# Column-divided products in groups, feed-forward units in pairs with 2 KB rows, compressed scores in float32r, and scheduler estimates with a margin

## The chip, the cores and the metric

The kernel runs on one core of one Trainium2 chip. The metric is the device time of one execution, in microseconds (us). The kernel before takes 1206.9 us (median of three runs, 1205.29 to 1207.57). In what follows PE is the matrix engine, DVE the vector engine, ACT the scalar engine, POOL is GpSimd, and SP is the engine whose queue issues the DMA transfers.

## The reference

Two layers work on 256 tokens of width 1024. Each layer is a half-step SwiGLU, token mixing, and a second half-step SwiGLU, each behind an RMS norm that is modulated by a vector `c`; a last RMS norm follows.

```
def swiglu(h, w_in, w_out):                    # w_in 1024 x 5632, w_out 2816 x 1024
    gate, up = jnp.split(h @ w_in, 2, axis=-1)
    return (jax.nn.silu(gate) * up) @ w_out

def token_mix(h, w_in, ...):                   # w_in 1024 x 3360
    (qkv, z, b_raw, a_raw, q_n, kc, vc, ks, vs, kw, vw, g_raw) = split_cols(h @ w_in, IN_SIZES)
    y_gdn = gated_deltanet(...)                # 4 heads of 128, triangular solves in chunks
    y_nsa = native_sparse_attention(...)       # 8 heads of 64, 2 groups of keys
    return jnp.concatenate([y_gdn, y_nsa], axis=-1) @ w_out

# in native_sparse_attention: compressed keys (15 of them), one of its three branches
sc = jnp.einsum("bgrqn,bngd->...", qb, k_cmp) * scale
p_cmp = masked_softmax(sc, cmp_end[None, :] <= t[:, None])
o_cmp = p_cmp @ v_cmp
```

The modulation (`ada_w`, 1024 x 9216 for each layer) is a product of one row, so that its weights are read once and used once. All is float32.

## The kernel before, in words

All weights are read from memory once, in one stream of tiles of 128 x 1024 floats (512 KB), into ten buffers `raw`. ACT rounds a tile to float32r (`hi`), DVE subtracts it from the tile (`lo`), and PE multiplies with both: a float32 product x·w is made of three float32r products, xh·wh, xl·wh and xh·wl, that add up in one PSUM bank. In the names of the profile a product `bank<-hh,lo` has the normed tokens' high part `hh` as the moving side and the weights' low part `lo` as the side that is loaded; `hl,hi` and `hh,hi` are the other two. There are four buffers each for `hi` and for `lo`, and eight PSUM banks of 128 x 512 floats.

The modulation's weights (`ada_w`) go through the same `raw` buffers, between the others; their products are made by DVE (`ada<-raw,cond,ada`), ACT and POOL (`adb<-adb,raw`), as a column sum that PE only finishes.

In the feed-forward part a unit is 256 columns of the gates and the same 256 of the values. Its four tiles (two halves of the rows, gates or values) have rows of 256 floats, 1 KB, in memory. A unit uses two banks, and `ffn_act` makes silu(gate) times value from each, split again into parts `aa`. The functions `split_mm` and `early_mm` issue the three products of one weight block directly behind each other:

```
        PE.matmul(o, wh, xh, start=first, stop=False, skip_group_check=True)
        PE.matmul(o, wh, xl, start=False, stop=False, skip_group_check=True)
        PE.matmul(o, wl, xh, start=False, stop=last, skip_group_check=True)
```

In the mixing part, products whose output has only 32 or 64 rows use a quarter or a half of the array's columns, and neighbours on other columns can run at once ("narrow" products below): the attention's values (`bank<-pt,vp`, 64 rows), sums over heads, the corners of the triangular inverses, the compression of keys, and the last step of the modulation. The scores with compressed keys (`bank<-KC,QS`) are float32 products of 16 columns; a mask is added by a product with the identity (`bank<-cmask,identb`).

The order of all this is not the order of the code. The kernel is first recorded; a list scheduler (`Program.schedule`, `forward`, `backward`, `estimate`) then walks through the recorded instructions along estimates of their times, picks for each engine the ready one with the longest way to the end, gives tiles their buffers, and issues everything in that order. So every instruction comes from one line of the profile, L546. The estimates decide the order on all engines, which queue in that order.

Of the kernel before, what the change touches and what calls it, by code (L numbers as in the profile page):

```python
# [6 lines left out]
F32 = mybir.dt.float32  # L7
# [40 lines left out]
def const_arrays():  # L48
    """Masks and index patterns that depend on the shapes alone."""
# [39 lines left out]
DMA_START, DMA_DONE, DMA_BYTES, DMA_RING = 1100, 950, 360.0, 8  # L89
# [20 lines left out]
class Instr:  # L110
    """A recorded instruction."""
# [5 lines left out]

    def operands(self):
        """(writes, access pattern) of each operand in memory."""
        for k, a in list(enumerate(self.args)) + list(self.kw.items()):  # L120
            if is_ap(a):
                yield k in (0, "out", "accum_out"), a
# [9 lines left out]
class LogicalTile:  # L132
    """A tile of the recorded program: one use of one of the slots of its tag."""
# [23 lines left out]


class Slots:
    """The slots of a tag. A tile may take one before tiles that precede it in the program only if all of them  # L160
    still get theirs when the rest of the program goes on in its own order."""
# [57 lines left out]
def wait_end(engine, end, other):  # L219
    """When an engine may reuse the place of a tile that another was done with at end."""  # L220
    if engine == "dma":
        return end + DMA_DONE
    return end + (REUSE[engine] if engine == other else HOP.get((engine, other), 200))


class Program:
    def __init__(self, tc, trace=None):
# [3 lines left out]
        self.in_order, self.last_dma, self.boost = False, None, 0  # L231
# [3 lines left out]
    # -- recording --  # L235
# [17 lines left out]
    def region(self, ap):  # L253
        """(tile, first partition, end, bits of the columns)"""
# [21 lines left out]
    def record(self, engine, fn, args, kw):  # L276
        x = Instr(len(self.instrs), engine, fn, args, kw)
# [5 lines left out]
        for w, r in sorted((u for u in uses if u[1]), key=lambda u: u[0]):  # L283
# [21 lines left out]
        if engine == "tensor":  # L305
            # products keep their order within a bank, as one start flag may stand for several of them
            b = args[0].tensor.name
            if b in self.last_pe:
                before.setdefault(self.last_pe[b], False)
            self.last_pe[b] = x  # L310
# [10 lines left out]
    def estimate(self, x):  # L321
        """Sets the time that the instruction holds its engine, and that of its transfer."""
# [3 lines left out]
        x.table, x.transfer = None, 0  # L326
# [96 lines left out]
    def forward(self):  # L423
# [28 lines left out]
        while len(order) < len(self.instrs):  # L452
# [29 lines left out]
            if switch(x):  # L482
                cost += TABLE_LOAD
                table = x.table[0]
# [1477 lines left out]
```

## Time and profile before

| | |
|---|---|
| median of three runs | 1206.9 us (1205.29 to 1207.57) |
| span of the profiled execution, from its first to its last instruction | 1203.7 us; the median lies 3.2 us above it |
| PE busy | 1160.3 us, 96% of the span |
| DVE busy | 958.1 us, 80% |
| ACT busy | 669.8 us, 56% |
| POOL busy | 219.6 us, 18% |
| read from memory | 256.09 MB, 215 GB/s over the span |

The profile has one execution. Engine times are busy times; matmuls are pipelined, so that one lasts longer in the trace than the distance to the next. How fast PE works is read from how many matmuls start in a stretch, or from the distance of two starts. The granted clock (PEclk) is the share of 2.4 GHz that PE got.

### The profile page before, as it was taken

The page shows a single profiled execution, that of the slowest core. Times are in us where ns is not written, and L with a number is a line of the kernel's source. Part 1 is how long each engine was busy: PE and PEld are TensorE (multiplying, and loading weights), DVE is VectorE, ACT ScalarE, POOL GpSimd, SP SyncE. Part 2 cuts the span into 40 slices and gives each one's busy share as a digit, 9 for nine tenths or more (in the row PEclk, how much of TensorE's full clock was granted, in tenths as well). Part 3 has the DMA queues.
Part 4 walks back from the last instruction along what each step waited for, and adds up shares of the span by engine and source line. Part 5 has one row for each costly group of instructions (what it writes and reads, how often), then busy time and mean ns, then how long its engine had stood idle before and what let it go on. Part 6 is the DMA issues. An engine that isn't in the chain of part 4 may idle for free.

```text
span 1203.7 us, 24132 instructions
## 1 busy us (share of the span) xinstructions
PE 1160.3 (96%) x9450; PEld 1080.6 (90%) x9451; DVE 958.1 (80%) x1716; ACT 669.8 (56%) x1177; POOL 219.6 (18%) x184
## 2 busy tenths in 40 slices
PE   8998989999999999999999999999999999999997
PEld 3698989997988899999999999998797879999997
DVE  3699899898987699988978877999998669855543
ACT  2456446555585556556545454556657556644444
POOL 2033343220001233113221110233100013200001
PEclk9999999999999999999999999999999999999999
DMA  9879999985424378987976887988562235756540
GB/s 333 292 218 313 293 303 308 287 254 171 132 54 123 118 225 294 301 272 227 319 224 187 284 265 221 314 283 283 157 192 55 71 102 181 255 172 193 181 145 36
DMA packets 230758, 259.89 MB, mean 216 GB/s; under 512 B 16130, under 2 KB 190836, under 8 KB 230644
## 3 DMA queue, kind: packets, MB, share of 16 engines
q1 hardware_dynamic: 230644, 258.35, 68.0%
q8 instruction: 74, 1.21, 0.4%
q14 instruction: 40, 0.33, 0.1%
HBM read 256.09 MB, written 2.23 MB: 215 GB/s over the span
## 4 chain that ended last, share of the span: by engine, by line
PE 72%; DVE 16%; DMA 4%; issue 3%; ACT 3%; POOL 1%; DVEq 0%; POOLq 0%; ACTq 0%; SPq 0%
PE bank L546 72%; DVE lo L546 7%; DVE ada L546 2%; ACT hi L546 2%; DMA raw<-in_ffn_w_out_dram 1%; DMA raw<-in_ada_w_dram 1%; DVE qT L546 1%; DVE aa L546 1%; POOL adb L546 1%; DMA raw<-in_ffn_w_in_dram 1%; DMA w<-in_cmp_w_k_dram 1%; DVE av L546 0%; DVE hl L546 0%; DVE KL L546 0%; DVE Pt L546 0%
## 5 line engine op out<-in xcount | busy, mean ns | idle before, releaser
L546 DVE TENSOR_TENSOR lo<-raw,hi 128x1024 fp32r<-128x1024 f32 (+3 forms) x340 | 420.2, 1254 | 119.6 <-ACT hi L546 86.4
L546 ACT ACTIVATE hi<-raw 128x1024 fp32r<-128x1024 f32 (+3 forms) x340 | 344.6, 1028 | 282.1 <-PE bank L546 233.2
L546 PE MATMUL bank<-hh,lo 128*128 128x256 f32 x1440 | 380.2, 285 | 10.4 <-DVE lo L546 10.3
L546 PE MATMUL bank<-hl,hi 128*128 128x256 f32 x1440 | 385.0, 284 | 0.6 <-DVE hl L546 0.6
L546 PE MATMUL bank<-hh,hi 128*128 128x256 f32 x1440 | 384.0, 283 | 1.6 <-ACT hi L546 1.0
L546 PEld LDWEIGHTS bank<-hh,lo 128*128 128x128 f32 x1440 | 260.2, 189 | 14.4 <-DVE lo L546 13.9
L546 PEld LDWEIGHTS bank<-hh,hi 128*128 128x128 f32 x1440 | 264.1, 189 | 4.7 <-issue 1.7
L546 PEld LDWEIGHTS bank<-hl,hi 128*128 128x128 f32 x1440 | 264.2, 189 | 1.2 <-DVE hl L546 0.8
L546 PE MATMUL bank<-aa,hi 128*128 128x256 f32 x1408 | 247.7, 281 | 2.9 <-ACT hi L546 2.5
L546 PEld LDWEIGHTS bank<-aa,hi 128*128 128x128 f32 x1408 | 212.5, 189 | 3.4 <-ACT hi L546 2.7
L546 PE MATMUL bank<-aa,lo 128*128 128x256 f32 x704 | 188.4, 283 | 8.5 <-DVE lo L546 8.5
L546 POOL TENSOR_TENSOR adb<-adb,raw 128x512 f32<-128x512 f32 x65 | 98.4, 1514 | 305.2 <-ACT raw L546 283.9
L546 PEld LDWEIGHTS bank<-aa,lo 128*128 128x128 f32 x704 | 129.5, 189 | 11.2 <-DVE lo L546 11.1
L546 DVE SCALAR_TENSOR_TENSOR ada<-raw,cond,ada 128x512 f32<-128x512 f32 x131 | 111.1, 848 | 4.5 <-DMA raw<-in_ada_w_dram 3.6
L546 POOL TENSOR_TENSOR nS<-nS,nsq 128x256 f32<-128x256 f32 x42 | 42.5, 1013 | 257.8 <-ACT nS L546 184.6
L546 ACT ACTIVATE aa<-av 128x256 fp32r<-128x256 f32 x88 | 36.0, 412 | 60.7 <-DVE av L546 60.5
L546 POOL TENSOR_TENSOR ada<-ada,adb 128x512 f32<-128x512 f32 x28 | 49.7, 1773 | 104.6 <-DVE ada L546 100.6
L546 PE MATMUL bank<-xl,hi 128*128 128x258 f32 (+1 forms) x224 | 62.3, 293 | 1.3 <-DVE xl L546 1.2
L546 PE MATMUL bank<-xh,hi 128*128 128x258 f32 (+1 forms) x224 | 60.5, 289 | 2.1 <-ACT xh L546 2.1
L546 PE MATMUL bank<-xh,lo 128*128 128x258 f32 (+1 forms) x224 | 61.4, 288 | 0.0
L546 DVE TENSOR_TENSOR aa<-av,aa 128x256 fp32r<-128x256 f32 x88 | 48.5, 554 | 10.9 <-ACT aa L546 10.9
L546 PEld LDWEIGHTS bank<-xl,hi 128*128 128x128 f32 x224 | 41.6, 190 | 7.1 <-issue 4.2
(308 smaller groups left out, 1620.9 us busy)
## 6 DMA issues: line engine op xcount, KB each, us to landing
raw<-in_ffn_w_in_dram SPq DMA_DIRECT2D x172, 512.0 KB, 4.8
raw<-in_ada_w_dram SPq DMA_DIRECT2D x144, 512.0 KB, 4.9
raw<-in_ffn_w_out_dram SPq DMA_DIRECT2D x64, 512.0 KB, 4.6
raw<-in_mix_w_in_dram SPq DMA_DIRECT2D x40, 512.0 KB, 5.0
raw<-in_ffn_w_out_dram SPq DMA_DIRECT2D x32, 384.0 KB, 4.3
raw<-in_mix_w_out_dram SPq DMA_DIRECT2D x8, 512.0 KB, 4.2
raw<-in_mix_w_out_dram SPq DMA_DIRECT2D x16, 256.0 KB, 4.5
raw<-in_mix_w_in_dram SPq DMA_DIRECT2D x8, 408.0 KB, 3.8
```

What stands on the lines that cost most here:

```text
L546: r = getattr(getattr(self.tc.nc, x.engine), x.fn)(*map(bind, x.args), **{k: bind(a) for k, a in x.kw.items()})
```

## The change

Five things change.

1. `split_mm` and `early_mm` become `split_products` and `early_products`: for all blocks of a weight tile first the two products with `hi`, then all products with `lo`.
2. The feed-forward units after the first ones go in pairs: 512 columns, four banks, tiles of 2 x 512 floats for each partition, so that a row in memory is 2 KB. 152 of the 172 loads of `ffn_w_in` have this form.
3. Narrow products are recorded as a group (`PE.together`), which the scheduler places as one.
4. The scores with compressed keys: keys in a high and a low part side by side (`KC`, made by ACT and DVE in place of copies by DVE), one float32r product of 32 columns for each head in place of a float32 one of 16, and the mask and the sum of both parts by two additions on DVE (`cs`) in place of the product with the identity. The queries' high and low part lie on different halves of the partitions, as before.
5. The scheduler's estimates: 12% on DVE's and ACT's, 8% on transfers, transfers by rows, costs for a pause of PE, for a change between full and narrow products, and for DVE beside POOL.

```
+SLACK = {"vector": 1.12, "scalar": 1.12, "gpsimd": 1.0, "sync": 1.08}
+REFILL, DIVIDE, SHARED = 100, 95, 500
...
+        x.port = (x.engine == "vector" and not psum and sum(free_size(a) > 64 for a in aps[1:]) > 1)
-            x.transfer = size / DMA_BYTES / min(1, run / 512)
+            x.transfer = size / run * (PACKET + run / PACKET_BYTES) / 16
...
+        x.cost *= SLACK.get(x.engine, 1)
+        x.transfer *= SLACK["sync"]
...
+            if x.port and clock["gpsimd"] > at:
+                cost += min(SHARED, clock["gpsimd"] - at)
             if x.engine == "tensor":
+                cost += (REFILL if at > clock["tensor"] + 20 else 0) + (DIVIDE if x.cols != cols else 0)
...
+    def together(self, body):
+        self.program.parts, whole = [], self.program.parts
+        body()
+        parts, self.program.parts = self.program.parts, None
+        self.program.record(self.name, "group", parts, {})
...
+        for u in range(single, 11, 2):
+            for h in range(2):
+                subs = [([dram("ffn_w_in", (l * 2 + i) * D * 2 * DFF + (2 * h + r) * 256 * 2 * DFF + s * DFF + u * 256,
+                               [[2 * DFF, 128], [128 * 2 * DFF, 2], [1, 512]])], (2, 512), "k c")
+                        for r in range(2) for s in range(2)]
+                w_item(("fp", l, i, u, h), subs)
...
+    def split_products(jobs):
+        for o, wh, _, xh, xl, first, _ in jobs:
+            PE.matmul(o, wh, xh, start=first, stop=False, skip_group_check=True)
+            PE.matmul(o, wh, xl, start=False, stop=False, skip_group_check=True)
+        for o, _, wl, xh, _, _, last in jobs:
+            PE.matmul(o, wl, xh, start=False, stop=last, skip_group_check=True)
...
+        for u in range(single, 11, 2):
+            qs = [bank() for _ in range(4)]
+            for h in range(4):
+                for s in range(2):
+                    wh, wl = take(("fp", l, i, u, h // 2), h % 2 * 2 + s)
+                    jobs = [[(qs[j][:, s * 256:(s + 1) * 256], wh[:, k, cut[j]], wl[:, k, cut[j]], hh[:, 2 * h + k],
+                              hl[:, 2 * h + k], h == 0 and s == 0 and k == 0, h == 3 and k == 1) for k in range(2)] for j in range(4)]
+                    for part in jobs if h == 3 and s == 1 else [sum(jobs, [])]:
+                        split_products(part)
+            for j in range(4):
+                ffn_act(2 * u + j, qs[j][:, 0:256], None, qs[j][:, 256:512], ah, al)
...
             for g in range(2):
                 for hf in range(2):
-                    V.tensor_copy(KC[hf * 64:(hf + 1) * 64, g], q[g * 64:(g + 1) * 64, 0:16])
+                    S.activation(KC[hf * 64:(hf + 1) * 64, g, 0], q[g * 64:(g + 1) * 64, 0:16], AF.Copy)
+                    V.tensor_tensor(KC[hf * 64:(hf + 1) * 64, g, 1], q[g * 64:(g + 1) * 64, 0:16],
+                                    fr(KC[hf * 64:(hf + 1) * 64, g, 0]), op=OP.subtract)
...
             def cmp_scores(b):
-                for r in range(4):
-                    for g in range(2):
-                        o = q[:, r * 32 + g * 16:r * 32 + (g + 1) * 16]
-                        PE.matmul(o, fr(QS[g][:, r, tok(b)]), KC[:, g], start=r == 0 and g == 0, stop=False, skip_group_check=True)
-                    PE.matmul(q[:, r * 32:(r + 1) * 32], identb, cmask[:, b], start=False, stop=True, skip_group_check=True)
+                def products():
+                    for r in range(4):
+                        for g in range(2):
+                            PE.matmul(q[:, (r * 2 + g) * 32:(r * 2 + g + 1) * 32], QS[g][:, r, tok(b)],
+                                      KC[:, g].rearrange("p y n -> p (y n)"), start=True, stop=True, skip_group_check=True)
+                PE.together(products)
+                V.tensor_tensor(qv, qp[:, :, 0], CC[:, C_CM + 32 * b:...], op=OP.add)
+                V.tensor_tensor(qv, qv, qp[:, :, 1], op=OP.add)
```

What the new order looks like on PE is shown at three places. The first is in the first feed-forward part, where PE multiplies unit after unit; numbers behind a name tell buffers apart, and `lo_1293` is made from `hi_1274`. Before:

```order
L546 MATMUL bank_1296<-hh_451,lo_1293 128x256
L546 MATMUL bank_1296<-hh_451,hi_1274 128x256
L546 MATMUL bank_1296<-hl_458,hi_1274 128x256
L546 MATMUL bank_1299<-hh_451,lo_1293 128x256
L546 MATMUL bank_1299<-hh_451,hi_1274 128x256
L546 MATMUL bank_1299<-hl_458,hi_1274 128x256
```

The product with `lo` stands directly behind the two with `hi` of its block, and those of the next block follow it. In the changed kernel, in the same part of the program on PE (`lo_1349` is made from `hi_1332`):

```order
L583 MATMUL bank_1174<-hh_425,hi_1332 128x256
L583 MATMUL bank_1174<-hl_430,hi_1332 128x256
L583 MATMUL bank_1142<-hh_425,lo_1349 128x256 x2
L583 MATMUL bank_1174<-hh_425,lo_1349 128x256 x2
L583 MATMUL bank_1142<-hh_425,hi_1354 128x256
L583 MATMUL bank_1142<-hl_430,hi_1354 128x256
```

The products with `lo` have moved behind all products with `hi` of their banks, in blocks.

The second place is PE in the first layer's mixing part, where the attention's values (`pt,vp`) begin. Before:

```order
L546 MATMUL bank<-KL,QS 128x256
L546 MATMUL bank<-pt,vp 64x128
L546 LDWEIGHTS identb
L546 MATMUL bank<-mask_qk,identb 128x2x128
L546 MATMUL bank<-pt,vp 64x128
L546 MATMUL bank<-CC,p 128x128 x4
L546 MATMUL bank<-pt,vp 64x128
L546 MATMUL bank<-CC,p 128x128
```

Each narrow product stands alone between full ones. In the changed kernel, at the first values of the same layer on PE:

```order
L583 MATMUL bank<-pct,VC 128x512
L583 MATMUL bank<-CC,p 128x128 x4
L583 MATMUL bank<-pt,vp 64x128 x4
L583 MATMUL bank<-qT,kT 128x256
L583 MATMUL bank<-CC,p 128x128
L583 MATMUL bank<-KH,QS 128x256
```

The four values of a unit have moved together.

The third place is PE at the first scores with compressed keys, in the same mixing part. Before:

```order
L546 MATMUL bank<-hl,hi 128x256
L546 MATMUL bank<-KC,QS 128x16
L546 LDWEIGHTS identb
L546 MATMUL bank<-cmask,identb 128x32
L546 MATMUL bank<-KC,QS 128x16 x2
```

In the changed kernel:

```order
L583 MATMUL bank<-hh,lo 128x256 x5
L583 MATMUL bank<-KH,QS 128x2x128
L583 MATMUL bank<-Vt,Pt 128x128 x4
L583 MATMUL bank<-KC,QS 128x32 x8
L583 MATMUL bank<-Vt,Pt 128x128 x4
```

The eight products of a block of tokens have moved together, and the products with the mask are gone.

## Rows read from the trace of the kernel before

**Rows 1.** The page's head and engines: busy us (share of the span) xinstructions.

```profile
span 1203.7 us, 24132 instructions
PE 1160.3 (96%) x9450; PEld 1080.6 (90%) x9451; DVE 958.1 (80%) x1716; ACT 669.8 (56%) x1177; POOL 219.6 (18%) x184
```

**Rows 2.** The page's chain that ended last, share of the span by engine.

```profile
PE 72%; DVE 16%; DMA 4%; issue 3%; ACT 3%; POOL 1%; DVEq 0%; POOLq 0%; ACTq 0%; SPq 0%
```

**Rows 3.** Stretches: PE, PEld, DVE, ACT, POOL busy (xinstructions), PEclk, DMA share, GB/s.

```profile
150.00:200.00 50.00, 44.48 (x354) 42.98 (x354) 47.24 (x65) 27.93 (x45) 20.13 (x13) 0.93 0.92 302
300.00:350.00 50.00, 49.42 (x458) 46.75 (x457) 44.73 (x138) 33.54 (x84) 0.40 (x4) 1.00 0.43 119
1050.00:1100.00 50.00, 50.00 (x430) 49.84 (x429) 28.23 (x40) 24.62 (x37) 0.00 (x0) 1.00 0.59 180
```

**Rows 4.** Waits of PE, whole run: us in total, times, longest.

```profile
PE bank L546 <- DVE lo L546: 19.1, 26, 2.1
PE bank L546 <- ACT hi L546: 3.4, 4, 2.5
```

**Rows 5.** Waits, from 60 to 250 us alone.

```profile
PE bank L546 <- DVE lo L546: 9.4, 9, 2.1
```

**Rows 6.** Timeline of PE: start, us, instruction xcount [idle before <-releaser].

```profile
172.12 0.28 PE L546 MATMUL bank<-hh,lo 128*128 128x256 f32 x1
174.88 0.50 PE L546 MATMUL bank<-aa,hi 128*128 128x256 f32 x2 [2.48 <-ACT hi L546]
...
177.09 0.58 PE L546 MATMUL bank<-hh,lo 128*128 128x256 f32 x1 [1.59 <-DVE lo L546]
177.46 0.41 PE L546 MATMUL bank<-hh,hi 128*128 128x256 f32 x1
177.68 0.41 PE L546 MATMUL bank<-hl,hi 128*128 128x256 f32 x1
```

**Rows 7.** Timeline of DVE, around the same time.

```profile
169.61 1.51 DVE L546 TENSOR_TENSOR aa<-av,aa 128x256 fp32r<-128x256 f32 x1
...
177.06 0.41 DVE L546 TENSOR_TENSOR aa<-av,aa 128x256 fp32r<-128x256 f32 x1
```

**Rows 8.** Stretches of 5 us, columns as in rows 3.

```profile
165.00:170.00 5.00, 5.00 (x45) 5.00 (x44) 4.49 (x6) 3.80 (x7) 3.64 (x4) 1.00 0.97 313
...
175.00:180.00 5.00, 3.41 (x16) 3.21 (x17) 5.00 (x8) 0.00 (x0) 0.34 (x1) 0.54 1.05 343
180.00:185.00 5.00, 5.00 (x42) 4.85 (x40) 3.48 (x5) 3.88 (x7) 0.95 (x1) 0.78 1.08 359
```

**Rows 9.** A group of PE by form: xcount | busy us, mean ns | idle before.

```profile
L546 PE MATMUL bank<-KC,QS 128*128 128x16 f32 x64 | 8.2, 251 | 0.0
```

**Rows 10.** Timeline of PE at scores with compressed keys.

```profile
320.93 0.18 PE L546 MATMUL bank<-cmask,identb 128*128 128x32 bf16 x1
320.96 0.60 PE L546 MATMUL bank<-KC,QS 128*128 128x16 f32 x4
321.40 0.18 PE L546 MATMUL bank<-cmask,identb 128*128 128x32 bf16 x1
```

**Rows 11.** Timeline of PE at values; a narrow product is two records.

```profile
355.58 0.43 PE L546 MATMUL bank<-pt,vp 128*64 128x128 f32 x2
355.95 0.66 PE L546 MATMUL bank<-CC,p 128*128 128x128 f32 x4
```

**Rows 12.** Timeline of PE at a whole unit of values.

```profile
385.98 0.66 PE L546 MATMUL bank<-pt,vp 128*64 128x128 f32 x8
386.57 0.39 PE L546 MATMUL bank<-KH,QS 128*128 128x256 f32 x1
386.79 0.28 PE L546 MATMUL bank<-KL,QS 128*128 128x256 f32 x1
```

**Rows 13.** DMA issues: xcount, KB each, us from issue to landing.

```profile
raw<-in_ffn_w_in_dram SPq DMA_DIRECT2D x172, 512.0 KB, 4.8
raw<-in_ada_w_dram SPq DMA_DIRECT2D x144, 512.0 KB, 4.9
```

More of the change, by code (lines that the diff above doesn't have):

```diff
@@ L116, in __init__ @@
         self.start = self.end = 0.0
+        self.parts = [Instr(i, engine, *x) for x in args] if fn == "group" else [self]
     def operands(self):
-        for k, a in list(enumerate(self.args)) + list(self.kw.items()):
-            if is_ap(a):
-                yield k in (0, "out", "accum_out"), a
+        for x in self.parts:
+            for k, a in list(enumerate(x.args)) + list(x.kw.items()):
+                if is_ap(a):
+                    yield k in (0, "out", "accum_out"), a
     def hop(self, other, data=True):
@@ L276, in record @@
     def record(self, engine, fn, args, kw):
+        if self.parts is not None:
+            self.parts.append((fn, args, kw))
+            return
         x = Instr(len(self.instrs), engine, fn, args, kw)
@@ L305, in record @@
         if engine == "tensor":
[L307 to L310, printed above, removed]
+            for b in {y.args[0].tensor.name for y in x.parts}:
+                if b in self.last_pe:
+                    before.setdefault(self.last_pe[b], False)
+                self.last_pe[b] = x
         if engine == "sync" and self.in_order:
@@ L321, in estimate @@
     def estimate(self, x):
+        if x.fn == "group":
+            for y in x.parts:
+                self.estimate(y)
+            x.cost, x.cols, x.table, x.transfer, x.port = sum(y.cost for y in x.parts), x.parts[0].cols, None, 0, False
+            return
         aps = [a for _, a in x.operands()]
@@ L451, in forward @@
         window, cold, busy = 0, True, {}
+        cols = 128
         while len(order) < len(self.instrs):
@@ L611, in full, with SINGLE @@
         return v.rearrange(f"p ({pat}) -> p {pat}", **dict(zip(pat.split(), shape)))
+    def SINGLE(l, i):
+        early = MID[2 * l + i] if l or i else EARLY
+        return early + (11 - early) % 2
     def ffn_in_items(l, i):
-        for u in range(11):
+        single = SINGLE(l, i)
+        for u in range(single):
             subs = [([dram("ffn_w_in", (l * 2 + i) * D * 2 * DFF + h * 512 * 2 * DFF + s * DFF + u * 256,
@@ L833, in fin, with columns @@
                 q = bank()
-                for j in range(4):
-                    PE.matmul(q[32 * j:32 * j + 32, 0:8], sel, ar.rearrange("p a c -> p (a c)")[:, j::4], start=True, stop=True)
+                def columns():
+                    for j in range(4):
+                        PE.matmul(q[32 * j:32 * j + 32, 0:8], sel, ar.rearrange("p a c -> p (a c)")[:, j::4], start=True, stop=True)
+                PE.together(columns)
                 c = slice(4 * p - 4, 4 * p + 4)
@@ L900, in trunk @@
     mask_qk = cst.tile([128, 128], BF16, name="mask_qk")
-    cmask = cst.tile([128, 2, 32], BF16, name="cmask")
     LM = cst.tile([128, 2, 128], U8, name="LM")
@@ L1075, in ffn_body @@
         if startup:
-            while items[st["next"][0]][1] != ("fi", 0, 0, EARLY):
+            while items[st["next"][0]][1] != ("fp", 0, 0, EARLY, 0):
                 produce()
@@ L1085, in ffn_body @@
         nst.pop("rbs")
-        for u in range(early, 11):
-            if between and 2 * u in between:
-                between[2 * u]()
+        single = SINGLE(l, i)
+        for u in range(early, single):
             qs = [bank(), bank()]
@@ L1354, in head_sums, with heads @@
                 q = bank()
-                for h in range(4):
-                    PE.matmul(q[h * 32:(h + 1) * 32, 0:T], ones[:, 0:32], sq[:, h], start=True, stop=True)
+                def heads():
+                    for h in range(4):
+                        PE.matmul(q[h * 32:(h + 1) * 32, 0:T], ones[:, 0:32], sq[:, h], start=True, stop=True)
+                PE.together(heads)
                 r = tmp([128, T], F32, "hs")
@@ L1770, in values, with products @@
                 b, r, y = units[u]
-                for j in range(2):
-                    for g in range(2):
-                        yy, kt, x = (j, 0, 2 * j + g) if b == 0 else (y, j, 2 * g + j)
-                        PE.matmul(O[b][g * 64:(g + 1) * 64, r * 128:(r + 1) * 128], vp[:, kt, yy, g], pt[:, x * 128:(x + 1) * 128],
-                                  start=False, stop=j == 1 and (b == 0 or y == 1), skip_group_check=True)
+                def products():
+                    for j in range(2):
+                        for g in range(2):
+                            yy, kt, x = (j, 0, 2 * j + g) if b == 0 else (y, j, 2 * g + j)
+                            PE.matmul(O[b][g * 64:(g + 1) * 64, r * 128:(r + 1) * 128], vp[:, kt, yy, g], pt[:, x * 128:(x + 1) * 128],
+                                      start=False, stop=j == 1 and (b == 0 or y == 1), skip_group_check=True)
+                PE.together(products)
             def norm_out(b):
@@ L1784, in norm_out, with heads @@
                 q = bank()
-                for r in range(4):
-                    PE.matmul(q[r * 32:(r + 1) * 32, 0:128], BO, osq[:, r * 128:(r + 1) * 128], start=True, stop=True)
+                def heads():
+                    for r in range(4):
+                        PE.matmul(q[r * 32:(r + 1) * 32, 0:128], BO, osq[:, r * 128:(r + 1) * 128], start=True, stop=True)
+                PE.together(heads)
                 sr = tmp([128, 128], F32, "nsr")
```

143 lines of the change are left out of this document (75 added, 68 removed).

## The prediction

> **What bounds the kernel now.** I read the page's engines first: PE is busy for 1160.3 of 1203.7 us [rows 1], and the chain that ended last is 72% PE, 16% DVE and 4% DMA [rows 2]. So time is won where PE idles or works slowly, and hardly anywhere else. A busy PE may still be slow, so next come the stretches: in the second layer's last feed-forward part 430 matmuls start in 50 us, one each 50/430 = 0.116 us, and nothing holds PE up; from 150 to 200 us it is 354 [rows 3]. In that stretch DVE is busy for 47.2 of 50 us and the DMA share is 0.92: PE is fed by engines that are nearly full. The list of PE's waits says by whom: 19.1 us on `lo`, in 26 waits, and 3.4 us on `hi` [rows 4]; 9.4 of the 19.1 us lie between 60 and 250 us [rows 5]. The rest of the forecast is about four things: these waits, the clock that one of them costs, narrow products, and the compressed scores.
>
> **Compressed scores.** Before, 64 records of `KC,QS` [rows 9]. Four of them take 321.40 - 320.96 = 0.44 us, so 0.11 each, and a mask product 0.03 [rows 10]. There are 16 of these (four for each of two blocks of tokens, two layers): 64 x 0.11 + 16 x 0.03 = 7.5 us. After: 32 float32r products of 32 columns, which the trace doesn't show. They lie between 0.03 (the mask's 32 columns) and 0.116 (256 columns of float32r), so 1.0 to 3.7 us together. I take 0.11, the step of the same loaded side (`QS`, 128 columns) with few columns: 3.5 us. **4.0 us** saved, bounds 3.8 to 6.5. They count in full, since PE is busy for 49.4 of 50 us around them [rows 3]. ACT's eight roundings of `KC` and DVE's eight small additions lengthen the way to the scores; PE's projection products cover that. Without this cover, four blocks would each wait for two more short DVE instructions, 0.41 us or less each [rows 7]: 3 us.
>
> **Narrow products.** Counting along PE's order, narrow products come in 123 runs between full ones before, and in 89 after: 34 excursions fewer. A lone narrow product takes 355.95 - 355.58 = 0.37 us until the next full one starts [rows 11]. Four together take 386.57 - 385.98 = 0.59 us, 0.15 each, and the first full one behind them takes 0.22 in place of 0.116, so that a way back costs 0.10 [rows 12]. An excursion less thus saves 0.37 - 0.15 = 0.22 us: **7.5 us** for 34. Bounds: 0.10 each (the way back alone), 3.4 us, and 0.37 each, 12.6 us. These matmuls stand in PE's own queue, so the saving is on the path wherever PE has other work, and the mixing part has (49.4 of 50 us).
>
> **`lo` behind all of `hi`.** A DVE subtraction for a whole tile takes some 1.2 us, and PE now asks for `lo` eight products (median over 344 tiles, by PE's order) after the first use of `hi`, in 85 tiles at most two products after it. In the changed order it is 15 products, and for no tile fewer than three. Fifteen products are 15 x 0.116 = 1.7 us, against a mean wait of 19.1/26 = 0.73 us [rows 4]. So a wait for `lo` goes where DVE has time and was merely asked too early. That holds for the 19.1 - 9.4 = 9.7 us outside of 60 to 250 us, which I count in full. In 60 to 250 us DVE is full, and a product that waits less for `lo` soon waits for the next `hi`: of the 9.4 us I count a quarter, 2.3 us. **12.0 us**; bounds 0 (all waits move to `hi`) and 19.1. What is queued behind a product with `lo` is all of PE, as before. `hi` buffers come free earlier and `lo` buffers no later, so ACT isn't held longer.
>
> **The clock.** At 172.1 to 177.1 us PE waits 2.48 us for `hi` and 1.59 us for `lo` [rows 6]. Then the granted clock is 0.54 and 0.78 in two stretches of 5 us [rows 8], which is half speed (1.2 GHz) for part of each: two matmuls start 0.22 us apart [rows 6]. Work lost: 5 x 0.46 + 5 x 0.22 = 3.4 us. Why the waits came: DVE instructions take 1.51 us that otherwise take 0.41 [rows 7], while POOL is busy for 3.64 of 5 us [rows 8]. The Trainium skill (GPSIMD Engine Reference, Specifications) says that POOL's interfaces to on-chip memory are shared with DVE and that DVE instructions with two inputs there contend. This trace agrees, with 1.10 us added to `aa<-av,aa`; by the rule the change, which only lets its planner reckon with 0.5 us for it, leaves the contention, and the sum would lack the term that follows. From the rows alone: the new order puts other instructions side by side, so that this stall is gone or not with even chances; I take half of the loss, **1.7 us**, bounds 0 and 3.4 + 2.5 (with the wait for `hi`).
>
> **2 KB rows.** A load of 512 KB lands in 4.8 us with 1 KB rows (`ffn_w_in`) and in 4.9 us with 2 KB rows (`ada_w`) [rows 13]. I count 0. The loads lie beside PE's work except where the DMA share is above 0.9; 2% (4.9 against 4.8) of the 150 us between 100 and 250 is 3 us to either side.
>
> **Pairs and margins.** A pair holds four of eight banks, so that the next one can start in the other four; 0. The margin and all else that the new order brings has no row. PE idles 43.4 us in all [rows 1], of which 22.5 are the waits in rows 4; I count 0, and bound it by half of the other 21 us, 10 us to either side.
>
> **Sum.** 4.0 + 7.5 + 12.0 + 1.7 = 25.2 us. 1203.7 - 25.2 = 1178.5 us of span, and 3.2 us for the distance of span and median: 1182 us.
>
> **Rivals.**
>
> *DVE sets the pace.* Then all waits for `lo` become waits for `hi`, and the clock falls as before: only 4.0 + 7.5 us remain, 1195 us. For it: DVE's 47.2 of 50 us at 150 to 200, and that PE's longest wait in this part is for `hi` [rows 3, 6]. Against it: half of the waits lie where DVE has time (28 of 50 us busy in a quiet stretch) [rows 3]. 22%.
>
> *More goes than I count.* All waits for `lo`, the clock and its wait for `hi`, and 3 us by faster loads: 4.0 + 7.5 + 19.1 + 5.9 + 3 = 39.5, 1167 us. For it: fewer pauses feed on themselves, since each one makes the buffers that DVE and ACT wait for come free later. 17%.
>
> *Banks, slower than before.* There are 20 pairs, five in each feed-forward part. If a norm, a modulation column or the last unit still holds a bank when a pair starts, PE waits until ACT and DVE have emptied it, and PE's queue holds all behind that product. At the longest wait for `lo` seen, 2.1 us [rows 4], that is 42 us against 25 gained: 1224 us. It decides from 25.2/20 = 1.3 us for each pair on. Against it: the banks of the pair before last are 192 x 0.116 = 22 us old by then, and ACT has 44% of its time idle [rows 1]. 11%.
>
> *Nothing comes of it.* The new order loses elsewhere what these terms gain (the bound of 10 us and the DVE rival together): within 0.2% of before, which is about what a measurement of this kernel can tell from no change, 1204.5 to 1209.3. 5%.
>
> **Chances.** The forecast, 1174 to 1190 us, has 45%; with 22, 17, 11 and 5% for the rivals that is all. Faster: 45 + 22 + 17, less 2 for the tail of the DVE rival that ends near 1205: 82%. Same: 6%. Slower: 12%. Eight in ten: from 1164, below the second rival's value, to 1204, which takes in the first rival and its spread of 10 us; what is left out is the slow side and a little of the fast one.
>
> **What would show it.** In the profile after: the sum of PE's waits for `lo` falls from 19.1 to some 7 us, and those for `hi` stay under 10; there are 32 records of `KC,QS` and no `cmask`, with starts 0.11 us apart; values come as eight records in 0.6 us; no stretch after the first 50 us has a granted clock below 1; the stretch of 150 to 200 us starts 380 matmuls or more where it had 354. Wrong would be: waits for `hi` or for transfers of 15 us and more, a wait of PE for ACT or DVE at the start of pairs, or as many matmuls per stretch as before.

## The result and the profile after

On one chip the changed kernel took 1188.4 us (median of 4 runs, 1187.5 to 1190.1) and the kernel before 1207.2 us (4 runs): a ratio of 0.985, with an interval of 0.983 to 0.986. The forecast was 1182 us, with a range of 1174 to 1190 (45%) and a wider one of 1164 to 1204 (eight in ten); the measured time lies in both. The profiled execution has a span of 1186.8 us; before it was 1203.7.

The head and the engines of the page, and its chain by engine, as in [rows 1, 2]:

```profile
span 1186.8 us, 24089 instructions
PE 1143.4 (96%) x9402; PEld 1075.6 (91%) x9403; DVE 946.6 (80%) x1723; ACT 669.0 (56%) x1185; POOL 224.0 (19%) x184
...
PE 77%; DVE 11%; issue 4%; ACT 3%; DMA 3%; POOL 2%; DVEq 0%; POOLq 0%; SPq 0%; ACTq 0%
```

PE is busy 17 us less, as much as the span is shorter, and DVE holds 11% of the chain in place of 16%. That looks like a plain success of PE's side. It isn't one, as a table by stages shows. A stage ends with the last product of a feed-forward part (the last with `aa`) or of a mixing part (the last with `yh`); the columns are us, PE busy (xmatmuls), PEclk, DMA share, GB/s. Before:

```profile
0.00:250.10 250.10, 233.15 (x1763) 0.98 0.91 295
250.10:424.20 174.10, 170.26 (x1417) 1.00 0.46 134
424.20:623.40 199.20, 194.59 (x1618) 1.00 0.83 269
623.40:821.80 198.40, 192.77 (x1621) 1.00 0.82 261
821.80:1002.40 180.60, 176.18 (x1414) 1.00 0.47 138
1002.40:1194.70 192.30, 190.44 (x1605) 1.00 0.53 165
```

After:

```profile
0.00:233.10 233.10, 226.16 (x1772) 1.00 0.92 312
233.10:415.20 182.10, 170.05 (x1391) 0.97 0.44 130
415.20:610.70 195.50, 191.58 (x1612) 1.00 0.83 277
610.70:802.00 191.30, 190.84 (x1621) 1.00 0.81 265
802.00:988.30 186.30, 173.10 (x1391) 0.95 0.47 141
988.30:1177.60 189.30, 188.70 (x1604) 1.00 0.51 165
```

The second and the fifth line are the mixing parts. The four feed-forward parts together fell from 840.0 to 809.2 us, 30.8 us. The two mixing parts rose from 354.7 to 368.4 us, 13.7 us, although PE has less to do there. PE idles 25.2 us there (368.4 - 343.2) where it idled 8.3. And the granted clock is 0.97 and 0.95 in place of 1.00: in six stretches of 27.3 us together it is at half speed (1.2 GHz). PE is busy for 25.7 us of these, so that its busy time would be some 330 us at full speed (an estimate, 343.2 - 25.7/2), against 346.4 before. PE's own work in the mixing parts thus fell by some 16 us, and idle time and clock took more than that.

PE's waits, whole run (us in total, times, longest), answering [rows 4]:

```profile
PE bank L583 <- ACT hh L583: 5.2, 7, 1.7
PE bank L583 <- DVE hT L583: 3.3, 2, 2.6
PE bank L583 <- DVE av L583: 2.7, 2, 1.5
PE bank L583 <- DVE lo L583: 2.3, 4, 1.2
...
PE bank L583 <- ACT hi L583: 1.9, 4, 0.6
```

The wait for `lo` is almost gone (19.1 before), and the one for `hi` has not taken its place (3.4 before). Many small waits for other tiles, most of them in the mixing parts, have come. The stretches of [rows 3]:

```profile
150.00:200.00 50.00, 46.43 (x397) 45.49 (x396) 48.17 (x72) 29.18 (x48) 21.81 (x14) 1.00 0.94 310
300.00:350.00 50.00, 46.98 (x438) 41.93 (x438) 45.11 (x135) 38.25 (x105) 0.60 (x6) 0.97 0.24 67
...
1050.00:1100.00 50.00, 50.00 (x426) 50.00 (x426) 27.57 (x33) 23.83 (x33) 0.00 (x0) 1.00 0.58 187
```

From 150 to 200 us 397 matmuls start where it was 354, with DVE and the transfers as full as before: PE isn't fed by a faster DVE there; the same work is laid out differently in time. From 300 to 350 us, where the prediction saw PE busy for 49.4 of 50 us and so counted each saved product, it is now busy for 47.0 (the mixing part starts 17 us earlier, so that this is not quite the same piece of it).

Compressed scores and values, by PE's timeline (start, us, instruction xcount); before in [rows 10 to 12]:

```profile
315.44 1.04 PE L583 MATMUL bank<-KC,QS 128*128 128x32 f32 x8
316.33 0.36 PE L583 MATMUL bank<-Vt,Pt 128*128 128x128 f32 x1
...
341.01 0.66 PE L583 MATMUL bank<-pt,vp 128*64 128x128 f32 x8
341.60 0.70 PE L583 MATMUL bank<-qT,kT 128*128 128x256 f32 x2
```

Eight scores in 0.89 us, 0.11 each, and four values (eight records) in 0.59 us.

What a pause in a mixing part looks like now, in the second layer. PE's timeline (in brackets idle time before it, and what ended it):

```profile
895.77 0.45 PE L583 MATMUL bank<-Tt,NT 128*32 128x32 f32 x16
896.79 0.45 PE L583 MATMUL bank<-Tt,NT 128*32 128x32 f32 x16 [0.58 <-ACT Tt L583]
...
899.37 0.73 PE L583 MATMUL bank<-Vt,Pt 128*32 128x32 f32 x16 [0.94 <-ACT Pt L583]
...
902.16 1.09 PE L583 MATMUL bank<-CC,Vt 128*128 128x128 f32 x4 [0.58 <-DVE csm L583]
```

The chain of waits in the same place (start, us, what):

```profile
897.97 1.07 ACT sq L583
...
899.05 0.27 ACT Pt L583
...
899.64 0.32 ACT pc L583
...
899.98 0.29 DVE csm L583
900.27 1.13 DVE lo L583
901.40 0.03 issue
901.43 0.29 DVE Vt L583
```

And two stretches (columns as in [rows 3]):

```profile
895.00:900.00 5.00, 3.24 (x73) 2.41 (x71) 4.61 (x15) 4.73 (x10) 0.00 (x0) 1.00 0.00 0
900.00:905.00 5.00, 4.42 (x33) 3.12 (x28) 4.35 (x11) 1.58 (x3) 0.00 (x0) 0.71 0.34 111
```

PE idles while ACT and DVE (4.73 and 4.61 of 5 us busy) pass short steps of the triangular inverses (`Tt`, `Pt`, `Vt`) and of the attention (`pc`, `csm`) to each other; a square of 1.07 us on ACT and a weight tile's subtraction of 1.13 us on DVE stand in that chain's way. Behind the pause the granted clock falls to 0.71.

### The profile page after: what moved, and what is told of

The parts are those of the page before. It is cut to its first block, busy times and chain, and to the rows that moved or that the text cites. A ratio compares the mean times of both kernels' runs of the same rounds, so it can differ in the third digit from the quotient of the medians.

```text
span 1186.8 us, 24089 instructions
## 1 busy us (share of the span) xinstructions
PE 1143.4 (96%) x9402; PEld 1075.6 (91%) x9403; DVE 946.6 (80%) x1723; ACT 669.0 (56%) x1185; POOL 224.0 (19%) x184
## 4 chain that ended last, share of the span: by engine, by line
PE 77%; DVE 11%; issue 4%; ACT 3%; DMA 3%; POOL 2%; DVEq 0%; POOLq 0%; SPq 0%; ACTq 0%
PE bank L583 77%; DVE lo L583 4%; DMA raw<-in_ada_w_dram 1%; DVE ada L583 1%; DVE kT L583 1%; ACT hi L583 1%; POOL nS L583 1%; DMA raw<-in_mix_w_in_dram 1%; DVE hl L583 1%; POOL adb L583 1%; DVE Pt L583 1%; DVE gm L583 0%; DVE aa L583 0%; DVE NT L583 0%; DVE nt L583 0%
## 5 line engine op out<-in xcount | busy, mean ns | idle before, releaser
L583 PE MATMUL bank<-hh,hi 128*128 128x256 f32 x1440 | 355.1, 284 | 2.4 <-ACT hh L583 1.8
L583 PE MATMUL bank<-hl,hi 128*128 128x256 f32 x1440 | 351.0, 284 | 0.1
L583 PE MATMUL bank<-hh,lo 128*128 128x256 f32 x1440 | 274.2, 285 | 2.2 <-DVE lo L583 2.1
L583 PEld LDWEIGHTS bank<-hh,lo 128*128 128x128 f32 x1440 | 217.2, 190 | 5.3 <-DVE lo L583 3.0
L583 PE MATMUL bank<-aa,hi 128*128 128x256 f32 x1408 | 205.7, 281 | 4.2 <-DVE av L583 2.7
L583 PEld LDWEIGHTS bank<-aa,hi 128*128 128x128 f32 x1408 | 185.7, 189 | 5.1 <-issue 3.0
L583 POOL TENSOR_TENSOR adb<-adb,raw 128x512 f32<-128x512 f32 x65 | 104.8, 1613 | 314.4 <-ACT raw L583 272.0
L583 PE MATMUL bank<-aa,lo 128*128 128x256 f32 x704 | 125.1, 282 | 0.5 <-DVE lo L583 0.2
L583 PEld LDWEIGHTS bank<-aa,lo 128*128 128x128 f32 x704 | 102.5, 188 | 1.6 <-DVE lo L583 1.5
L583 ACT ACTIVATE raw<-raw,cond 128x512 f32<-128x512 f32 x65 | 44.4, 712 | 7.0 <-DMA raw<-in_ada_w_dram 6.7
```

Source lines behind the costliest of these rows:

```text
L583: r = getattr(getattr(self.tc.nc, y.engine), y.fn)(*map(bind, y.args), **{k: bind(a) for k, a in y.kw.items()})
```

## The experiments

Feed-forward and mixing are sums of the four and two stages, in us; `lo` is PE's wait for `lo`, changes are those from a full to a narrow product in the mixing parts. The end, 9 to 10 us in all of them, is left out.

| kernel | ratio to before, interval | feed-forward | mixing | lo | changes |
|---|---|---|---|---|---|
| before | 1 | 840.0 | 354.7 | 19.1 | 89 |
| after | 0.985, 0.983 to 0.986 | 809.2 | 368.4 | 2.3 | 59 |
| e1_lo_behind_hi | 1.010, 1.008 to 1.013 | 839.1 | 367.1 | 14.8 | 95 |
| m_planner_alone | 1.010, 1.007 to 1.012 | 823.2 | 384.2 | 4.1 | 105 |
| e4_interleaved | 0.994, 0.992 to 0.996 | 828.4 | 361.6 | 11.7 | 52 |
| e7_oldest | 1.006, 1.004 to 1.008 | 846.1 | 355.4 | 24.5 | 54 |
| e3_nomargin | 1.006, 1.004 to 1.008 | 826.6 | 377.7 | 10.1 | 59 |
| b_margins_alone | 1.005, 1.004 to 1.006 | 835.6 | 366.0 | 5.0 | 52 |
| e2_nogroup | 1.006, 1.004 to 1.008 | 813.4 | 388.9 | 1.9 | 126 |
| e5_singles | 0.983, 0.981 to 0.984 | 814.3 | 361.2 | 3.3 | 53 |
| j_margin_111 | 0.990, 0.988 to 0.991 | 816.0 | 369.1 | 8.7 | 52 |
| b_margin_120 | 0.982, 0.980 to 0.983 | 818.1 | 357.1 | 2.5 | 58 |
| f1_same_places | 1.175, 1.171 to 1.179 | 996.7 | 405.0 | 29.5 | 87 |
| f4_same_places | 1.347, 1.344 to 1.350 | 1175.8 | 440.2 | 187.0 | 61 |

How far the plan itself is a throw of dice was asked of j_margin_111:

```
-SLACK = {"vector": 1.12, "scalar": 1.12, "gpsimd": 1.0, "sync": 1.08}
+SLACK = {"vector": 1.11, "scalar": 1.11, "gpsimd": 1.0, "sync": 1.08}
```

> The kernel after with the margins of DVE and ACT at 1.11 in place of 1.12: a step too small to mean anything by itself, to see how far planning anew moves the time. If each planning is a throw, it lands anywhere from 1183 to 1200 us, with the mixing parts 5 us or more from 368; the single differences of 5 to 10 us between the other kernels then tell nothing. If it is within 2 us of 1188, they tell something.

1195.5 us, 7 us more than after, for a step of 0.01. The feed-forward parts moved by 6.8 us, the mixing parts by 0.7. The mixing parts alone are no steadier: in after, j_margin_111, b_margin_120 and e5_singles, which differ in a margin or in the feed-forward parts only, they take 357.1 to 369.1 us, 12 us apart. So a difference of 7 us in time, or of 12 us in the mixing parts, between two kernels that were planned anew says nothing of the edit by itself; what follows rests on larger differences, or on several pairs of kernels that agree.

**What took the waits for `lo` away.** The new order of products alone, in the kernel before (e1_lo_behind_hi):

```
+        for o, wh, _, xh, xl, first, _ in jobs:
             PE.matmul(o, wh, xh, start=first, ...)
             PE.matmul(o, wh, xl, start=False, ...)
-            PE.matmul(o, wl, xh, start=False, stop=last, ...)
+        for o, _, wl, xh, _, _, last in jobs:
+            PE.matmul(o, wl, xh, start=False, stop=last, ...)
```

> The kernel before with one edit: in the units of weights, all products with hi stand ahead of those with lo. Theory A (the new order of products took away the waits for lo and, with them, most of the 30.8 us that the feed-forward parts gained): the feed-forward parts, 840 us before, come to 815 to 825, PE's waits for lo fall from 19 to under 5 us, the time to about 1187 to 1194. Theory B (the planner's new estimates, margins and price for contention took them away): feed-forward parts stay within 5 us of 840, time 1202 to 1210. Theory C (the pairs with 2 KB rows took them away): as B. The mixing parts stay at 355 us by A; if they rise to 362 or more here too, their loss of 13.7 us does not come from groups or margins.

```profile
PE bank L546 <- DVE lo L546: 14.8, 21, 1.5
```

Theory A failed: 1220 us, feed-forward parts as before, and `lo` is still waited for. PE asks later, and the planner puts the subtraction later too: from the end of ACT's `hi` to the end of DVE's `lo` of the same tile it is 1.52 us in the kernel before (median over 344 tiles, paired in order) and 2.21 us here. In the two kernels below it is 1.53 (old order of products, new estimates) and 1.50 (e4_interleaved).

In the kernel after it is 2.19 as well, although PE hardly waits there, so that this median doesn't tell what took the waits away. The room tells more, from the end of a tile's `lo` on DVE to PE's first product with it (paired by the order in which each kernel's own scheduler issues them). It is 0.1 us or less for 36 of the 344 tiles before, and still for 31 here, for 36 in e7_oldest and for 45 in e3_nomargin, which all plan without margins. In the eight kernels with margins that were planned in the usual way it is so for 8 to 24 tiles, 12 of them in the kernel after.

The mixing parts rose to 367.1 us here, with nothing but the order of products changed. By the test that the expectation set (362 or more), what the kernel after loses there need not come from groups or margins.

The planner's estimates alone, in the kernel before (m_planner_alone):

```
+REFILL, DIVIDE, SHARED = 100, 95, 500
+SLACK = {"vector": 1.12, "scalar": 1.12, "gpsimd": 1.0, "sync": 1.08}
...  (and the times of transfers and of narrow products)
```

> The kernel before with the planner's new estimates, price for contention and margins, and none of the other edits. Theory P: feed-forward parts fall from 840 to 825 or 830 us, about as in the kernel after with the old order of products (828), waits for lo to about 12 us. Theory A (the order of products is what pays): they stay within 5 us of 840. The mixing parts have no groups here: if groups are worth 20 us there, they rise to 375 or more; if not, 355 to 368.

```profile
PE bank L558 <- DVE lo L558: 4.1, 11, 1.0
```

Theory P came true in the main: waits for `lo` fall to 4.1 us, further than the 12 expected, and the feed-forward parts by 16.8 us, with the old order of products. The kernel is slower all the same, by 29.5 us in its mixing parts, which have no groups; 375 us or more there was to mean that groups are worth some 20 us under these estimates.

The kernel after with the old order of products (e4_interleaved: the first diff the other way), and with all of the old estimates (e7_oldest):

> The kernel after with the old order of products (hi, lo and hi with the other half of the weights in turn, tile by tile). Theory A: waits for lo come back, 10 to 19 us of them, and the time rises by 10 to 20 us to 1198 to 1208, all of it in the feed-forward parts. Theories B and C: within 5 us of 1188. If the margins leave enough room ahead of lo, it is B.

> The kernel after with all of the planner's estimates as they were before (no margins, no price for contention or for changing between full and narrow products, the old times of transfers and of narrow products); products, groups, pairs and compressed scores stay. Theory A (order of products): feed-forward parts at 820 us or less. Theory P (it is the order and the plan together): 825 to 840, as with the margins alone taken away (827). In the mixing parts: if the new estimates are what makes PE wait there, they come to 350 us or less, time about 1185; if the groups leave PE with less work than the chain of DVE and ACT takes, they stay at 365 to 380, time 1200 to 1220.

```profile
PE bank L583 <- DVE lo L583: 24.5, 22, 2.9
```

e4_interleaved loses 19.2 us in the feed-forward parts, as theory A wanted, and gains 6.8 us in the mixing parts, which it didn't; e7_oldest, which has every edit but the estimates, loses 36.9 us in the feed-forward parts, more than either theory allowed, and waits more for `lo` than the kernel before. Read as a square, the feed-forward parts take 840 us with neither, 839 and 846 with the order of products alone, 823 and 828 with the estimates alone, and 809 to 818 with both (five kernels). By the means (840, 842.6, 825.8 and 814.2) the estimates are worth 14 us with the old order of products and 28 with the new one. The order is worth some 12 us, with 5 us between the nearest two kernels, and only under the new estimates.

Which of the estimates? The margins taken away (e3_nomargin, all of `SLACK` at 1.0), and the margins alone (b_margins_alone, the other estimates as before):

> The kernel after with the margins on the planner's times set to 1.0. Theory M (the margins spread the mixing parts' work so that PE waits and its clock falls): the mixing parts fall from 368 to about 357 us and the time to about 1177. Theory B (the margins are what keeps PE from waiting in the feed-forward parts): the feed-forward parts rise from 809 to 820 or more, time 1198 or more. By the prediction, which counted the margins at nothing: 1184 to 1193.

> The kernel after with the margins, but with all other estimates of the planner as they were before (no price for contention or for changing between full and narrow products, the old times of transfers and of narrow products). So far the feed-forward parts took 809 to 818 us wherever the new estimates and the new order of products came together, 827 without the margins and 846 with no new estimate; the mixing parts took 355 us with the old estimates and 357 to 369 with the new ones (378 with the new ones without margins). Theory Q (the margins help the feed-forward parts, the other estimates harm the mixing parts): feed-forward 812 to 822, mixing 352 to 360, time 1176 to 1188, the fastest so far. Rival R (the margins themselves stretch the mixing parts, or the other estimates are needed in the feed-forward parts too): mixing 362 or more, or feed-forward 825 or more, time 1190 to 1210.

Without the margins the feed-forward parts lose 17.4 us, without the others 26.4. So both are needed there. Theory M failed, since the mixing parts rose without the margins, to 377.7 us, and theory Q, that the others could be left out, failed too: 1213 us. Against e7_oldest, which has neither, the margins alone take the waits for `lo` from 24.5 to 5.0 us, but only 10.5 us off the feed-forward parts; the others alone take 19.5 us off them. Which of the others does it was not taken apart. One of them, the price for DVE beside POOL, doesn't do what its name says: `aa<-av,aa` takes 0.42 us (median) or up to 1.53 us in the kernel after (count, shortest, median and longest in ns):

```profile
L583 DVE TENSOR_TENSOR aa<-av,aa x88: 403/420/1531, 72.2 to 1124.0; 128x256 fp32r<-128x256 f32 x88
```

It takes over 0.6 us in 14 of 88 cases before, in 13 after, and in 9 in e7_oldest, which has no such price: the long cases stay. In these three kernels each of them lies beside busy time of POOL. By the rule that the prediction took from the Trainium skill (GPSIMD Engine Reference, Specifications) they would; the trace agrees.

Two kernels were to take the planner out: they put the products of a piece of weights into the places that the plan of the other order of products had given them, with every other engine's queue as it was. f1_same_places does this in the kernel before, f4_same_places in the kernel after:

```
+    for y in dst.instrs:
+        if y.unit is not None:
+            pos[y] = units[y.unit].pop()      # the unit's own places, in the new order
...
+        # where the places would wait for each other, the next product that can go takes its turn
+        y = min(can, key=lambda y: pos[y]) if can else next(x for x in reversed(queues["tensor"]) if before[x] <= done)
```

> The kernel before with the new order of products, but not planned anew: every instruction of the other engines keeps its place in its queue, and the products of a piece of weights share the places that they had, those with lo last. Theory A (asking later for lo pays by itself): PE's waits for lo fall from 19 to under 5 us, the feed-forward parts from 840 to about 828 us, the mixing parts stay at 355 us, time 1192 to 1197. Theory P (the order pays only where the planner has left DVE room): the waits go over to hi and to others, feed-forward parts stay within 3 us of 840, time 1203 to 1210. In both, the 12 us that planning the same edit anew cost in the mixing parts do not come.

> The kernel after with the old order of products (hi, hi, lo in turn), not planned anew: all else keeps its place. Theory A: waits for lo of 10 us or more come back, feed-forward parts rise from 809 to 820 or more, time 1198 to 1206. Theory P: the margins have put DVE's subtractions so early that hardly a wait comes back; within 4 us of 1188.

Both were far off, 1417 and 1627 us. PE's waits in f4_same_places:

```profile
PE bank L583 <- DVE lo L583: 187.0, 153, 8.2
```

They don't measure the order of products: where places were in each other's way other products moved too, and PE's queue is a different one throughout. The 153 waits of 1.2 us for `lo` speak against theory P too, which had hardly a wait come back, but with PE's queue so different that isn't shown. What the order of products would bring in an unchanged plan stays open.

**Pairs with 2 KB rows.** The kernel after with units one by one (e5_singles):

```
-        return early + (11 - early) % 2
+        return 11
```

> The kernel after with units one by one and rows of 1 KB. Theory C (pairs and longer rows carry a part of the feed-forward parts' gain): these rise from 809 by 10 us or more. By the prediction, which gave them nothing: they stay within 5 us of 809. The mixing parts may move by some 10 us either way, as planning anew has moved them so far.

1186.8 us, 0.983 against 0.985 for after, and feed-forward parts of 814.3 us, 5.1 us more. Theory C, which wanted 10 us or more, failed; 5 us are less than what planning anew moves. A load of `ffn_w_in` lands in 5.1 us there and in 4.7 us in the kernel after; PE waits for none of them in either.

**The mixing parts.** The kernel after without groups (e2_nogroup):

```
     def together(self, body):
-        self.program.parts, whole = [], self.program.parts
         body()
-        parts, self.program.parts = self.program.parts, None
-        self.program.record(self.name, "group", parts, {})
```

> The kernel after without the groups: narrow products are planned one by one. By the prediction's term (34 excursions of 0.22 us) it is 7.5 us slower, 1196, with about 120 changes from full to narrow products where the kernel after has 89. Theory G (groups hold PE in the mixing parts, which is where the half clock and the 13.7 us come from): it is faster by 5 to 10 us, 1178 to 1184, with mixing parts under 360 us and less than 14 us at half clock.

```profile
235.20:423.90 188.70, 183.80 (x1391) 0.99 0.43 127
...
812.00:1012.20 200.20, 189.83 (x1391) 0.97 0.45 133
```

1215 us. Theory G failed: groups don't hold PE up, without them the mixing parts take 20.5 us more. Counted from the first narrow product to the next full one, over the whole run, PE spends 72.6 us in 123 runs of narrow products before, 66.5 us in 88 runs after, and 93.1 us in 166 runs here. PE's idle time within these runs, 3.6, 8.5 and 10.0 us, is counted in. Under the new estimates the planner breaks ungrouped products up more than it did before (126 changes in the mixing parts against 89), and groups cure that.

Against the kernel before, no gain is left. e7_oldest has groups and the new compressed scores with the old estimates; its mixing parts:

```profile
252.60:425.50 172.90, 164.03 (x1398) 1.00 0.46 138
...
825.30:1007.80 182.50, 170.54 (x1391) 0.96 0.47 140
```

PE is busy for 334.6 us in place of 346.4, 11.8 us less, and idles 20.8 us in place of 8.3: the sum is 355.4 us, as before (354.7), and between what the two theories had for it. But e7_oldest has the new order of products too, which the kernel before lacks. The mixing parts of the three kernels that stand beside it, e1_lo_behind_hi, m_planner_alone and e4_interleaved, two lines each:

```profile
247.20:433.30 186.10, 178.12 (x1414) 0.99 0.45 131
834.80:1015.80 181.00, 175.78 (x1415) 1.00 0.48 141
...
241.80:429.60 187.80, 177.80 (x1418) 1.00 0.44 126
816.70:1013.10 196.40, 185.78 (x1409) 0.97 0.44 129
...
247.90:428.20 180.30, 167.33 (x1392) 0.98 0.45 131
818.60:999.90 181.30, 169.69 (x1391) 0.96 0.48 142
```

With the order of products and the estimates equal, groups and new scores (and pairs, which don't touch these parts) do show in the time: 11.7 us from e1_lo_behind_hi to e7_oldest, 22.6 us from m_planner_alone to e4_interleaved, and 20.5 us for the groups alone, from e2_nogroup to the kernel after. What took the gain, as far as these pairs tell, is the plan. The new order of products costs the mixing parts 12.4 us (before to e1_lo_behind_hi) and 6.8 (e4_interleaved to after), the new estimates cost them 29.5 (before to m_planner_alone) and 13.0 (e7_oldest to after). The smaller of these differences lie within or near the 12 us that planning anew moves these parts; but the three savings agree, and so do the four costs.

In all eight kernels with groups that were planned in the usual way PE idles some 20 us or more in the mixing parts, and none of them has these parts shorter than before: they take 355 to 378 us. The idle time isn't the groups' doing alone, since m_planner_alone idles 20.6 us there and e2_nogroup 15.3 without them. Why the new order and the new estimates make the plan of the mixing parts worse was not taken apart.

**A larger margin** (b_margin_120, 1.20 for DVE and ACT):

> The kernel after with the margins of DVE and ACT at 1.20 in place of 1.12. From 1.00 to 1.12 the time fell from 1215 to 1188 us. If room ahead of DVE's and ACT's results is what counts, it falls a little more, to 1178 to 1187, with less than 17 us of PE's waits and half clock in the mixing parts; if 1.12 has taken all there was, 1186 to 1195.

1186.2 us, the lowest median of all, with the mixing parts at 357 us. The time came as expected, but the sign that was to show why did not: PE idles 20 us in the mixing parts, with a clock of 0.99 and 0.97, where less than 17 us of waits and half clock together were expected. It and e5_singles lie below the kernel after in their medians, by 2.2 and 1.6 us and so by less than the 7 us that a meaningless step moves; no reason is claimed for them.

## Why the prediction was right, and where it was not

The time, the sign and the main place (waits for `lo` in the feed-forward parts) were right. The way to the number was half wrong: the feed-forward parts gained 30.8 us where 13.7 were counted, and the mixing parts lost 13.7 us where 11.5 were counted as gained. The sum came out near by luck, because errors of 17 us (feed-forward) and 25 us (mixing) had opposite signs.

*Compressed scores, 4.0 us.* The work was sized rightly: 32 records at 0.11 us, 3.5 us in place of 7.5. That they "count in full, since PE is busy for 49.4 of 50 us around them" was argued from a plan that didn't stay: in the changed kernel PE idles 25.2 us in the mixing parts. No run has the old scores with all else new. Together with the groups they show in the time between kernels of equal order and estimates (11.7 and 22.6 us, for 11.5 counted), and not against the kernel before.

*Narrow products, 7.5 us.* 34 excursions at 0.22 us were counted; measured are 35 runs fewer and 72.6 - 66.5 = 6.1 us, 0.17 each. Without PE's idle time inside the runs it is 69.06 - 58.02 = 11.04 us, 0.32 each, and against an ungrouped program under the same planner (83.1 - 58.0)/78 = 0.32 as well. So the work on PE was sized too low, within its bounds.

*`lo` behind all of `hi`, 12.0 us.* The effect was forecast as 19.1 down to some 7 us of waits; it was 2.3. The cause was given wrongly. "A wait for `lo` goes where DVE has time and was merely asked too early" supposes that DVE's place in the order stays when PE asks later. The planner moves DVE as well: with the order of products alone 14.8 and 24.5 us of waiting are left. It is the margins that leave room ahead of `lo`. That DVE has time outside of 60 to 250 us was misread too: the stretch given for it lies in the last feed-forward part, which holds 0.6 us of the waits, while 8.0 of the 9.7 us lie between 424 and 822 us, where DVE is busy for 341 of 398 us.

*Pairs and margins, 0.* The pairs were nothing, as far as 7 us can tell. "All else that the new order brings" at 0 is the step that failed. In the feed-forward parts the estimates bring 839 to 846 us down to 809 to 818, with the order of products the same; in the mixing parts the new order and the new estimates cost what groups and scores save, and more. The bound of 10 us to either side, half of PE's other idle time, was too small for both. It left out the term above it, which hangs on the same estimates, and that a new plan can add idle time as well as take it away.

PE's idle time in the feed-forward parts fell by 17.1 us, to 11.9, and its busy time by another 13.7. Of these 5.1 us are the clock (below). A pause also costs more than its idle time: matmuls take 0.28 us and follow each other in 0.116, so that up to 0.17 us of each pause stands in the profile as busy; with 24 pauses of over 0.05 us in place of 39 that makes up to 2.5 us, and the other 6 us are not accounted for. The Trainium skill (Perfetto Trace Analysis, Identifying the Most-Contended Engine) warns against judging by PE's busy share: it is no good measure of how close PE is to its limit, as matmuls are pipelined. This trace agrees, with a busy share of 96% before and after.

*The clock, 1.7 us.* The stall near 175 us is gone, with the 3.4 us that it cost, and so is a half-speed stretch near 25 us, worth 1.7: 5.1 us in the feed-forward parts, where none is left. "No stretch after the first 50 us with a clock below 1" failed: 0.97 and 0.95 in the mixing parts, some 14 us.

*2 KB rows, 0.* Right, as far as 7 us can tell (e5_singles).

*Rivals.* That DVE sets the pace fell: waits for `hi` went from 3.4 to 1.9 us with DVE as full as before. Banks at the start of pairs were no wait to speak of: `av`, which empties a bank, is waited for twice, 2.7 us in all. (There are 19 pairs, not the 20 that this rival counts: 152 loads, eight to a pair.) "More goes than I count" came true for the feed-forward parts alone. No rival named the mixing parts.

Open are which of the other estimates helps, what the order of products is worth in a fixed plan, what makes the plan of the mixing parts worse, and whether the mixing parts' clock would hold if PE were given filler work there, which wasn't tried.

## What to carry to other kernels

In a kernel whose order comes from a planner, an edit to one engine's work is an edit to every queue: undo each part alone, and run a change that means nothing, before a part is given credit. That an engine is busy doesn't prove that a saving on it counts, and a time that stays the same doesn't prove that it was lost: compare kernels that differ in that part alone. Here groups and scores look like nothing against the kernel before, and like 11.7 to 22.6 us between kernels of equal order and estimates. Margins on the estimated times of the engine that feeds decide whether a later request becomes a later delivery; here they took most of the waits away, but paid in full only together with the other estimates.

## What was not expected of the hardware

The cost of alternating between full and narrow products: 0.32 us of PE's busy time for each change back and forth, between e2_nogroup and the kernel after (25.1 us for 78) and between the kernels before and after (11.0 us for 35). And how readily the clock falls in the mixing parts: in the kernel after PE idles there for 25 of 368 us, 7%, no single wait longer than 2.6 us, and on top of that some 14 us are lost to stretches at half speed (1.2 GHz). With 8 us of idle time, before, nothing was lost; with 13 us, in e1_lo_behind_hi, 1.7 us; with 31 us, in e3_nomargin, 20.5. The idle time alone doesn't settle it: b_margin_120 and e5_singles idle 20 us each there and lose 6.8 and 13.7.
